# Moving one low half of weights per plain up tile to GpSimd, and setting the four convolution taps in one block

## The chip, the cores and the metric

The kernel runs on one core of one Trainium2 chip. The metric is the device time of one execution in microseconds (us), the median of several runs. Engines are named as in the profile: PE is TensorE (matmul), PEld its weight loads, DVE is VectorE, ACT is ScalarE, POOL is GpSimd, SP is SyncE. SP only issues DMAs here.

## The reference

A two-layer decoder trunk over 512 positions of width 1024. Layer 0 mixes positions with a gated MLP, layer 1 with sliding-window attention; both then run the same channel mixer, which is the part that the change touches, and a gated per-layer embedding. The channel mixer is a gated MLP with a causal depthwise convolution of width 3 between the up-projection and the activation; D_FF is 2816, so `w_up` has 5632 columns:

```python
def conv_ffn(xn, w_up, conv_w, conv_b, w_down):
    h = xn @ w_up
    hp = jnp.pad(h, ((0, 0), (CONV_WIDTH - 1, 0), (0, 0)))
    c = conv_b + sum(hp[:, t:t + S] * conv_w[t] for t in range(CONV_WIDTH))
    g, u = jnp.split(c, 2, axis=-1)
    return (jax.nn.silu(g) * u) @ w_down
...
for i in range(DEPTH):
    ...
    h = h + conv_ffn(rmsnorm(h, norm_ffn[i]), f_w_up[i], f_conv_w[i], f_conv_b[i], f_w_down[i])
```

Everything is float32, and the output is the normalised trunk, 512 x 1024.

## The kernel before, in words

**Products.** Each float32 product is made of three matmuls in the type fp32r: both operands are split into a high half (rounded to fp32r) and a low half (what is left), and the products high x high, high x low and low x high are added in PSUM. So every weight that TensorE uses must first be split.

**Weights.** All weights are planned ahead (L71 to L139) as a list of `pieces`, which are cut into `units` of at most 1024 columns. SP loads each piece into one of three raw buffers (`wraw`). `pump` (L179 to L206) prepares one unit after the other: ACT casts the high half (`wh`, L203), and then DVE subtracts, raw minus high, for the low half (`wl`, L204). There are four `wh` and four `wl` buffers (`WBUFS`), and whoever takes a unit first has units up to four ahead prepared. Some pieces are *woven*, that is, TensorE gets sums of quarters of the weights and so does seven products of half-size blocks where there were eight: for these, `weave` (L155 to L166) makes three sums on DVE in a buffer `wsum` (L163 to L165), and the piece has four units, three of up to 1024 columns and one of up to 512.

**The channel mixer** is `ffn` (L730 to L850). Its 22 up tiles (index j) are each 128 columns of the gate half and 128 of the other, for all 512 positions. They are worked in three parts: tiles 0 to 7, 8 to 15 and 16 to 21. Plain tiles are j = 0 to 6, 11, 13, 15 and 19, eleven to a layer: `up` (L737) takes two units, does 48 matmuls into two PSUM banks, and calls `gated` (L754). The other tiles are woven: `woven_up`, which ends in the same `gated`.

**`gated`** makes the convolution and the activation of a tile. For each half s: ACT writes `c_s`, the current position's tap with the bias, out of PSUM (L760); then DVE adds the two earlier positions, one instruction for each tap, which multiplies PSUM by a scalar and adds it to `c_s` (L762). Then ACT does silu of `c_0` (L768), and DVE multiplies by `c_1` (L769), which gives `a`.

**The end of a part.** Parts 0 and 1 close with the down-projection in woven form. Pairs of tiles are prepared by `Pair` (L504): sums of them on DVE (L518, L532 to L535), and their high and low halves `act` (the low halves on DVE at L312). Then TensorE runs first the next part's first up tile (8 or 16, woven; its two results are called `ux` and `uy`), without its `gated`, and after it `woven_add` (L593), whose two results are called `dx` and `dy` and whose first product uses `edge` and the first unit of `w_down`. That unit is number 59 at the end of part 0 and number 101 at the end of part 1; layer 1 has the same two ends with other numbers. Part 2 closes with plain products (`dense_add`). The last plain tile before the end of part 0 is tile 6 (tile 7 is woven), and before the end of part 1 it is tile 15.

**Order.** Nothing but the program sets the order on an engine: each engine runs its own list in the order in which the scheduler put it when the kernel was built, and waits, at an instruction, for whatever that instruction needs. `behind` holds an instruction behind another in that order, without a wait.

Of the kernel before, what the change touches and what calls it, by code (L numbers as in the profile page):

```python
# [8 lines left out]
F32 = mybir.dt.float32  # L9
F32R = mybir.dt.float32r  # L10
AF = mybir.ActivationFunctionType
ALU = mybir.AluOpType

P = 128
D = 1024
S = 512
# [36 lines left out]
def tile_yoco(ctx: ExitStack, tc: tile.TileContext, t, out: bass.AP, out_b: bass.AP):  # L53
# [83 lines left out]
                      [(ap, f"ah{q}", f"al{q}") for q in free[k0 : k0 + 4]] if c else None)  # L137

    units = [(i, q, lo, n) for i, p in enumerate(pieces) for q, (lo, n) in enumerate(p[2])]  # L139
    raws, ready, splits, sums = {}, {}, {}, {}  # L140
    state = {"raw": 0, "unit": 0, "next": 0, "tags": [0, 1, 2], "turn": 2, "pt": 0, "sent": {}}

    def behind(ins, front):

        tc.add_manual_dep(ins.ins, front.ins.name,
                          mybir.DependencyInfo(mybir.DependencyClass.NoSync, mybir.DependencyReason.DATA),
                          reason="order")

    def staged(name):
        tags = state["tags"]  # L150
# [28 lines left out]
    def pump(upto):  # L179
        while state["unit"] < min(upto, len(units)):  # L180
            i, q, lo, n = units[state["unit"]]
            load(i + 1)
            u = state["unit"]
            own = pieces[i][3]
            if own:
                pool, *tags = own[q]
                wh, wl = (pool.tile([P, n], F32R, tag=tg, name=f"own{u}_{tg}") for tg in tags)
            else:
                wh = wp.tile([P, UNIT], F32R, tag="wh", bufs=WBUFS, name=f"wh{u}")
                wl = wp.tile([P, UNIT], F32R, tag="wl", bufs=WBUFS, name=f"wl{u}")  # L190
            if i in woven:
                src = weave(i, q)
                hi, low = (x[:, :n].rearrange("p (b k m) -> p b k m", b=src.shape[1], m=P) for x in (wh, wl))
            elif i in paired:
                whole = raws[i][:, : pieces[i][1]].rearrange("p (c k n) -> p k c n", c=2, n=256)
                src = whole[:, lo // S : (lo + n) // S]
                hi, low = (x[:, :n].rearrange("p (k c n) -> p k c n", c=2, n=256) for x in (wh, wl))
            else:
                src, hi, low = raws[i][:, lo : lo + n], wh[:, :n], wl[:, :n]
            if u == 0:  # L200
                cast = nc.vector.tensor_copy(hi, src)
            else:
                cast = nc.scalar.copy(hi, src)  # L203
            state["split"] = splits[u] = cast, nc.vector.tensor_sub(low, src, hi.bitcast(F32))  # L204
            ready[u] = (wh, wl, n)
            state["unit"] += 1  # L206

# [74 lines left out]
    for i in range(IDLE):  # L282
        nc.tensor.matmul(ps, idle, idle.rearrange("p (o t) -> p o t", o=1).to_broadcast([P, 4, P]),
                         start=True, stop=True)
    minus_half = const.tile([P, S // 64], F32, name="minus_half")
    nc.vector.memset(minus_half, -0.5)
    ident = const.tile([P, P], F32, name="ident")
# [442 lines left out]
    def ffn(l, norm, nxt):  # L730
# [6 lines left out]
        def up(j, later=False):  # L737
            if j in UPS:
                return woven_up(j, later)
            parts = chunk(256, KD)  # L740
            pss = [psum(f"up{j}_{s}") for s in range(2)]
            if j:
                for s in range(2):
                    mm3(pss[s], parts, xs, s * P)
            else:
                for k, ((wh, wl, off), (xh, xl)) in enumerate(zip(parts, xs)):
                    for x, both in ((xh, (wh, wl)), (xl, (wh,))):
                        for s, ps in enumerate(pss):
                            for w in both:
                                nc.tensor.matmul(ps, w[:, off + s * P : off + (s + 1) * P], x,  # L750
                                                 start=k == 0 and x is xh and w is wh, stop=k == KD - 1 and x is xl)
            return pss if later else gated(j, pss)

        def gated(j, pss, fronts=()):  # L754
            cs = []
            for s, ps in enumerate(pss):
                col = s * NJ + j
                cw = [v("conv_w", (l * 3 + i) * 2 * NJ + col) for i in range(3)]
                c = tp.tile([P, S], F32, tag=f"c{s}", name=f"c{j}_{s}")
                nc.scalar.activation(c, ps, AF.Identity, bias=v("conv_b", l * 2 * NJ + col), scale=cw[2])  # L760
                for tap in (1, 2):
                    ins = nc.vector.scalar_tensor_tensor(c[:, tap:], ps[:, : S - tap], cw[2 - tap], c[:, tap:],  # L762
                                                         op0=ALU.mult, op1=ALU.add)
                    if fronts and tap == 1:
                        behind(ins, splits[fronts[s]][1])
                cs.append(c)
            a = tp.tile([P, S], F32, tag="sg", name=f"a{j}")
            box["silu"] = nc.scalar.activation(a, cs[0], AF.Silu)  # L768
            nc.vector.tensor_mul(a, a, cs[1])  # L769
            return a  # L770
# [866 lines left out]
```

## Time and profile before

| | |
|---|---|
| median of three runs | 1100.64 us (1100.06 to 1100.65) |
| span of the profiled execution | 1098.7 us |
| what the median is above the span | 1.9 us |
| PE busy | 1089.1 us (99%) |
| DVE busy | 959.0 us (87%) |
| ACT busy | 661.0 us (60%) |
| POOL busy | 125.0 us (11%) |
| instructions of PE, DVE, ACT, POOL | 6629, 1540, 1141, 192 |
| granted TensorE clock | full in each of 40 slices |

The profile is of one execution. Its span runs from the first instruction to the last; the time of an execution is taken outside of it. "Busy" is the time in which an engine has an instruction in work; matmuls follow each other in a pipeline and their ends overlap, so 99% says that TensorE nearly always had a next matmul, not that it was at its peak. A row of the timeline gives the start, the duration, engine, line and operation, output and inputs by the program's names without numbers, how many instructions were put together, and in brackets how long the engine was idle before them and what ended that. DVE's rows also overlap: the next instruction starts some 0.08 us before the row of the one ahead ends.

### The profile page before, as it was taken

What the parts mean: (1) busy time and instruction counts of PE and PEld (TensorE: products, weight loads), DVE (VectorE), ACT (ScalarE), POOL (GpSimd) and SP (SyncE); (2) the same over time, 40 slices, a digit from 0 to 9 for tenths busy, and PEclk for the clock granted to TensorE, in tenths of its full rate; (3) what the DMA queues carried; (4) which work ended last, traced back from release to release, by engine and by line L of the source; (5) the groups of instructions that cost most, each with busy time, mean ns of one, the idle gap of its engine ahead of it and who ended that gap; (6) DMA issues with size and microseconds to landing.
All of it is one profiled execution on the core that took longest, in us unless ns stands there. A gap on an engine that the chain in (4) does not pass through costs nothing.

```text
span 1098.7 us, 17476 instructions
## 1 busy us (share of the span) xinstructions
PE 1089.1 (99%) x6629; PEld 974.4 (89%) x6629; DVE 959.0 (87%) x1540; ACT 661.0 (60%) x1141; POOL 125.0 (11%) x192
## 2 busy tenths in 40 slices
PE   9999999999999999999999999999999999999997
PEld 7888988899998999988888887888999989999886
DVE  5588889999899989877988997799998999898887
ACT  5735666565676656655656775565655666567544
POOL 2200200000100010021114452000001000100200
PEclk9999999999999999999999999999999999999999
DMA  9621674125633267353234216441255333664534
GB/s 317 113 88 39 178 264 150 43 77 116 155 115 116 79 160 222 120 190 112 67 87 135 78 58 227 176 153 39 77 142 128 115 116 86 156 220 142 203 95 98
DMA packets 47508, 144.24 MB, mean 131 GB/s; under 512 B 13048, under 2 KB 18688, under 8 KB 36928
## 3 DMA queue, kind: packets, MB, share of 16 engines
q1 hardware_dynamic: 40560, 128.77, 35.6%
q0 software_dynamic: 5296, 9.70, 6.7%
q10 hardware_dynamic: 1568, 4.65, 1.1%
q8 instruction: 52, 0.85, 0.3%
q14 instruction: 32, 0.26, 0.1%
HBM read 116.89 MB, written 18.88 MB: 124 GB/s over the span
## 4 chain that ended last, share of the span: by engine, by line
PE 95%; DVE 2%; issue 1%; ACT 1%; DMA 0%; SPq 0%; POOLq 0%; POOL 0%; ACTq 0%
PE up L234 20%; PE ux L234 10%; PE dx L234 10%; PE uy L234 8%; PE dy L234 8%; PE d L234 6%; PE q L234 4%; PE gate L234 4%; PE u L234 4%; PE o L234 4%; PE up L750 2%; PE pv L1326 1%; PE v L244 1%; PE v L245 1%; PE v L246 1%; PE pin L234 1%
## 5 line engine op out<-in xcount | busy, mean ns | idle before, releaser
L204 DVE TENSOR_TENSOR wl<-wraw,wh 128x1024 fp32r<-128x1024 f32 (+2 forms) x198 | 217.3, 1102 | 42.8 <-ACT wh L203 41.9
L203 ACT CAST wh<-wraw 128x1024 fp32r<-128x1024 f32 (+2 forms) x197 | 182.8, 933 | 107.6 <-PE up L234 21.8
L203 ACT CAST wh<-wsum 128x1024 fp32r<-128x1024 f32 x84 | 88.3, 1052 | 62.7 <-issue 14.9
L204 DVE TENSOR_TENSOR wl<-wsum,wh 128x1024 fp32r<-128x1024 f32 x84 | 102.5, 1225 | 16.1 <-ACT wh L203 16.0
L762 DVE SCALAR_TENSOR_TENSOR c<-up,vec,c 128x511 f32<-128x511 f32 (+1 forms) x88 | 65.0, 744 | 2.4 <-ACT c L760 1.9
L234 PE MATMUL up<-nf10h,wh 128*128 128x512 f32 x160 | 62.3, 389 | 0.0
L234 PE MATMUL up<-nf00h,wh 128*128 128x512 f32 x160 | 62.3, 389 | 0.0
L234 PE MATMUL up<-nf10l,wh 128*128 128x512 f32 x160 | 62.3, 389 | 0.0
L234 PE MATMUL up<-nf00l,wh 128*128 128x512 f32 x160 | 62.3, 389 | 0.0
L234 PE MATMUL up<-nf00h,wl 128*128 128x512 f32 x160 | 62.1, 389 | 0.0
L234 PE MATMUL up<-nf10h,wl 128*128 128x512 f32 x160 | 62.0, 389 | 0.0
L600 POOL DMA_DIRECT2D saved<-head x16 | 13.9, 871 | 412.9 <-DVE head L720 412.9
L760 ACT ACTIVATE c<-up,vec 128x512 f32<-128x512 f32 x44 | 34.0, 777 | 31.8 <-PE up L234 26.6
L163 DVE TENSOR_TENSOR wsum<-wraw 128x1024 f32<-128x1024 f32 x42 | 51.2, 1220 | 0.6
L234 PE MATMUL ux<-t,wh 128*128 128x256 f32 x264 | 50.4, 283 | 0.0
L234 PEld LDWEIGHTS ux<-t,wh 128*128 128x128 f32 x264 | 41.2, 192 | 0.0
L234 PE MATMUL ux<-t,wl 128*128 128x256 f32 x132 | 37.4, 283 | 0.0
L234 PEld LDWEIGHTS up<-nf00h,wl 128*128 128x128 f32 x160 | 30.0, 188 | 6.2
L234 PEld LDWEIGHTS up<-nf10h,wl 128*128 128x128 f32 x160 | 30.0, 188 | 6.2
L234 PEld LDWEIGHTS up<-nf00l,wh 128*128 128x128 f32 x160 | 30.0, 188 | 6.2
L234 PEld LDWEIGHTS up<-nf10l,wh 128*128 128x128 f32 x160 | 30.0, 188 | 6.2
L234 PEld LDWEIGHTS up<-nf10h,wh 128*128 128x128 f32 x160 | 30.0, 188 | 6.0
(769 smaller groups left out, 3734.3 us busy)
## 6 DMA issues: line engine op xcount, KB each, us to landing
wraw<-in_w_up SPq DMA_DIRECT2D x44, 1024.0 KB, 5.6
wraw<-in_w_down SPq DMA_DIRECT2D x16, 1024.0 KB, 5.0
wraw<-in_w_gate SPq DMA_DIRECT2D x8, 1024.0 KB, 5.5
wraw<-in_w_down SPq DMA_DIRECT2D x8, 768.0 KB, 4.5
wraw<-in_w_u SPq DMA_DIRECT2D x4, 1024.0 KB, 9.4
wraw<-in_w_out SPq DMA_DIRECT2D x4, 1024.0 KB, 4.9
saved<-head POOLq DMA_DIRECT2D x16, 256.0 KB, 4.2
saved<-tail POOLq DMA_DIRECT2D x16, 256.0 KB, 4.1
```

The lines of the kernel that those rows point to most:

```text
L163: nc.vector.tensor_add(s[:, 0::3], g[:, 1:2].to_broadcast([P, 2, k, P]), g[:, 0::3])
L203: cast = nc.scalar.copy(hi, src)
L204: state["split"] = splits[u] = cast, nc.vector.tensor_sub(low, src, hi.bitcast(F32))
L234: return [nc.tensor.matmul(ps, w, x, start=first and j == 0, stop=last and j == len(todo) - 1, skip_group_check=onto) for j, (w, x) in enu ...
L244: nc.tensor.matmul(ps, xh[:, s], wh[:, a:b], start=st, stop=False)
L245: nc.tensor.matmul(ps, xl[:, s], wh[:, a:b], start=False, stop=False)
L246: nc.tensor.matmul(ps, xh[:, s], wl[:, a:b], start=False, stop=en)
L600: box["onto"] = nc.gpsimd.dma_start(x, y, accum_op=ALU.add)
L750: nc.tensor.matmul(ps, w[:, off + s * P : off + (s + 1) * P], x, start=k == 0 and x is xh and w is wh, stop=k == KD - 1 and x is xl)
L760: nc.scalar.activation(c, ps, AF.Identity, bias=v("conv_b", l * 2 * NJ + col), scale=cw[2])
L762: ins = nc.vector.scalar_tensor_tensor(c[:, tap:], ps[:, : S - tap], cw[2 - tap], c[:, tap:], op0=ALU.mult, op1=ALU.add)
L1326: nc.tensor.matmul(ps, lhs, rhs, start=j == 0, stop=j == len(todo) - 1)
```

## The change

In a plain up tile, the two halves of `gated` are taken together. ACT writes both `c_0` and `c_1` first. Then, at a higher priority for the scheduler, DVE copies one column of `c_1` to a small buffer `sign` (which nothing reads), and right behind it run the four taps in one block: first tap of `c_0`, first tap of `c_1`, second tap of `c_0`, second tap of `c_1`, each held behind the one ahead. One unit of weights that is prepared about then (the one that is two units beyond those which the tile has taken) gets its low half on GpSimd and not on VectorE, and this subtraction waits for the copy to `sign` with a semaphore. So 22 low halves of 128x1024, eleven in each layer, go from DVE to POOL, and DVE gets 22 copies of 128x1. Woven tiles keep the old `gated`.

```diff
+    def after(ins, front):
+
+        tc.add_manual_dep(ins.ins, front.ins.name,
+                          mybir.DependencyInfo(mybir.DependencyClass.Sync, mybir.DependencyReason.DATA),
+                          reason="start")
...
-            state["split"] = splits[u] = cast, nc.vector.tensor_sub(low, src, hi.bitcast(F32))
+            start = shadows.pop(u, None)
+            lows = (nc.gpsimd if start else nc.vector).tensor_sub(low, src, hi.bitcast(F32))
+            if start:
+                after(lows, start)
+            state["split"] = splits[u] = cast, lows
...
+    sign = const.tile([P, 1], F32, name="sign")
...
-            return pss if later else gated(j, pss)
-
-        def gated(j, pss, fronts=()):
+            return pss if later else gated(j, pss, shadow=True)
+
+        def gated(j, pss, fronts=(), shadow=False):
             cs = []
+            if shadow:
+                taps = []
+                for s, ps in enumerate(pss):
+                    col = s * NJ + j
+                    c = tp.tile([P, S], F32, tag=f"c{s}", name=f"c{j}_{s}")
+                    nc.scalar.activation(c, ps, AF.Identity, bias=v("conv_b", l * 2 * NJ + col),
+                                         scale=v("conv_w", (l * 3 + 2) * 2 * NJ + col))
+                    taps += [(c, ps, tap, v("conv_w", (l * 3 + 2 - tap) * 2 * NJ + col)) for tap in (1, 2)]
+                    cs.append(c)
+                with tc.high_priority():
+                    last = nc.vector.tensor_copy(sign, cs[1][:, :1])
+                    shadows[state["next"] + 2] = last
+                    for c, ps, tap, w in taps[::2] + taps[1::2]:
+                        ins = nc.vector.scalar_tensor_tensor(c[:, tap:], ps[:, : S - tap], w, c[:, tap:],
+                                                             op0=ALU.mult, op1=ALU.add)
+                        behind(ins, last)
+                        last = ins
+                a = tp.tile([P, S], F32, tag="sg", name=f"a{j}")
+                box["silu"] = nc.scalar.activation(a, cs[0], AF.Silu)
+                nc.vector.tensor_mul(a, a, cs[1])
+                return a
             for s, ps in enumerate(pss):
```

The line numbers shift with it: of what is named above, L163 to L165 become L169 to L171, L203 and L204 become L209 and L211, L312 becomes L323, L518 becomes L529, L532 to L535 become L543 to L546, L769 becomes L786 in a plain tile (L801 in a woven one). The copy is L777, the taps of the block are L780.

How DVE's list stands at two places. The names hold the tile (`c6_1` is the second half of tile 6, `act0_3_2` the third of the splits of pair 3 in part 0) or the unit (`wl59`), with a number behind it that is only a counter. The first place is DVE's list at the end of the last plain tile of part 0 in layer 0. Before:

```order
L762 SCALAR_TENSOR_TENSOR c6_0_2289<-up6_0_2239,vec_84,c6_0_2289 128x511
L312 TENSOR_TENSOR act0_2_2_2214<-act0_2u_2215,act0_2_2_2214 128x512
L762 SCALAR_TENSOR_TENSOR c6_0_2289<-up6_0_2239,vec_84,c6_0_2289 128x510
L204 TENSOR_TENSOR wl53_2309<-wsum26_2229,wh53_2308 128x1024
L204 TENSOR_TENSOR wl54_2313<-wraw26_2225,wh54_2312 128x512
L762 SCALAR_TENSOR_TENSOR c6_1_2293<-up6_1_2240,vec_84,c6_1_2293 128x511
L163 TENSOR_TENSOR wsum27_2345<-wraw27_2341 128x2x512
L762 SCALAR_TENSOR_TENSOR c6_1_2293<-up6_1_2240,vec_84,c6_1_2293 128x510
L164 TENSOR_TENSOR wsum27_2345<-wsum27_2345,wraw27_2341 128x512
L769 TENSOR_TENSOR a6_2297<-a6_2297,c6_1_2293 128x512
```

The same place on DVE in the changed kernel:

```order
L323 TENSOR_TENSOR act0_2_2_2221<-act0_2u_2222,act0_2_2_2221 128x512
L777 COPY sign_132<-c6_1_2298 128x1
L780 SCALAR_TENSOR_TENSOR c6_0_2296<-up6_0_2246,vec_84,c6_0_2296 128x511
L780 SCALAR_TENSOR_TENSOR c6_1_2298<-up6_1_2247,vec_84,c6_1_2298 128x511
L780 SCALAR_TENSOR_TENSOR c6_0_2296<-up6_0_2246,vec_84,c6_0_2296 128x510
L780 SCALAR_TENSOR_TENSOR c6_1_2298<-up6_1_2247,vec_84,c6_1_2298 128x510
L211 TENSOR_TENSOR wl54_2321<-wraw26_2232,wh54_2320 128x512
L786 TENSOR_TENSOR a6_2305<-a6_2305,c6_1_2298 128x512
L169 TENSOR_TENSOR wsum27_2353<-wraw27_2349 128x2x512
```

`wl53` has gone from DVE's list to POOL's. The two taps of `c6_0` and the half-size low `wl54`, which stood ahead of the first tap of `c6_1`, now stand with it or behind it.

The second place is DVE's list where the first units of the down-projection are prepared, at the end of part 0. Before:

```order
L312 TENSOR_TENSOR act0_3_0_2436<-a7_2433,act0_3_0_2436 128x512
L535 SCALAR_TENSOR_TENSOR act0_3u_2439<-act0_3u_2439,a7_2433 128x256
L312 TENSOR_TENSOR act0_3_1_2437<-act0_3t_2301,act0_3_1_2437 128x512
L204 TENSOR_TENSOR wl59_2486<-wraw28_2483,wh59_2485 128x1024
L312 TENSOR_TENSOR act0_3_2_2438<-act0_3u_2439,act0_3_2_2438 128x512
L204 TENSOR_TENSOR wl60_2520<-wsum28_2487,wh60_2519 128x1024
```

The same place on DVE in the changed kernel:

```order
L323 TENSOR_TENSOR act0_3_0_2444<-a7_2441,act0_3_0_2444 128x512
L546 SCALAR_TENSOR_TENSOR act0_3u_2447<-act0_3u_2447,a7_2441 128x256
L171 TENSOR_TENSOR wsum28_2495<-wsum28_2495,wraw28_2491 128x512
L323 TENSOR_TENSOR act0_3_1_2445<-act0_3t_2309,act0_3_1_2445 128x512
L323 TENSOR_TENSOR act0_3_2_2446<-act0_3u_2447,act0_3_2_2446 128x512
L211 TENSOR_TENSOR wl59_2494<-wraw28_2491,wh59_2493 128x1024
L211 TENSOR_TENSOR wl60_2528<-wsum28_2495,wh60_2527 128x1024
```

The split `act0_3_2` now stands ahead of `wl59`; the sum `wsum28` has only moved among work that stood ahead of `wl59` already. And at the end of part 1, on DVE before:

```order
L312 TENSOR_TENSOR act1_3_0_3843<-a15_3840,act1_3_0_3843 128x512
L535 SCALAR_TENSOR_TENSOR act1_3u_3846<-act1_3u_3846,a15_3840 128x256
L204 TENSOR_TENSOR wl101_3897<-wraw40_3894,wh101_3896 128x1024
L312 TENSOR_TENSOR act1_3_1_3844<-act1_3t_3775,act1_3_1_3844 128x512
L312 TENSOR_TENSOR act1_3_2_3845<-act1_3u_3846,act1_3_2_3845 128x512
```

There in the changed kernel:

```order
L323 TENSOR_TENSOR act1_3_0_3854<-a15_3851,act1_3_0_3854 128x512
L546 SCALAR_TENSOR_TENSOR act1_3u_3857<-act1_3u_3857,a15_3851 128x256
L323 TENSOR_TENSOR act1_3_1_3855<-act1_3t_3785,act1_3_1_3855 128x512
L170 TENSOR_TENSOR wsum40_3909<-wsum40_3909,wraw40_3905 128x512
L323 TENSOR_TENSOR act1_3_2_3856<-act1_3u_3857,act1_3_2_3856 128x512
L171 TENSOR_TENSOR wsum40_3909<-wsum40_3909,wraw40_3905 128x512
L211 TENSOR_TENSOR wl101_3908<-wraw40_3905,wh101_3907 128x1024
```

Here both splits `act1_3_1` and `act1_3_2` have moved ahead of the first unit's low half, `wl101`.

More of the change, by code (lines that the diff above doesn't have):

```diff
@@ L139, in tile_yoco @@
     units = [(i, q, lo, n) for i, p in enumerate(pieces) for q, (lo, n) in enumerate(p[2])]
-    raws, ready, splits, sums = {}, {}, {}, {}
+    raws, ready, splits, sums, shadows = {}, {}, {}, {}, {}
     state = {"raw": 0, "unit": 0, "next": 0, "tags": [0, 1, 2], "turn": 2, "pt": 0, "sent": {}}
```

## The prediction

> **What bounds the kernel now.** I read the page first: busy shares, and the shares of the chain that ended last.
>
> ```profile
> PE 1089.1 (99%) x6629; PEld 974.4 (89%) x6629; DVE 959.0 (87%) x1540; ACT 661.0 (60%) x1141; POOL 125.0 (11%) x192
> ...
> PE 95%; DVE 2%; issue 1%; ACT 1%; DMA 0%; SPq 0%; POOLq 0%; POOL 0%; ACTq 0%
> ```
>
> TensorE is the bound. So a shorter list on VectorE is worth only what TensorE waits for VectorE today. That is the view of the waits, for PE:
>
> ```profile
> PE idle L283 <- DVE minus_half L286: 1.1, 1, 1.1
> PE v L952 <- ACT n00h L307: 0.4, 1, 0.4
> PE uy L234 <- ACT side L805: 0.3, 2, 0.2
> ```
>
> The columns are us in total, times, longest. The first two are at the start of the program. No wait for a low half (L204) or for a tap (L762) is listed at all. Then I looked at where VectorE has room and where not, with busy times by stretch (start:end, length, PE, PEld, DVE, ACT and POOL busy, clock, DMA):
>
> ```profile
> 156.00:231.00 75.00, 75.00 (x338) 62.31 (x337) 70.05 (x111) 43.48 (x61) 0.00 (x0) 1.00 0.28 94
> 231.00:256.00 25.00, 24.85 (x207) 24.59 (x206) 24.68 (x37) 18.22 (x31) 0.00 (x0) 1.00 0.29 99
> 364.00:380.00 16.00, 16.00 (x134) 15.86 (x133) 15.22 (x23) 12.08 (x20) 0.00 (x0) 1.00 0.38 131
> ```
>
> The first stretch is the plain tiles of part 0 in layer 0: DVE has 5 us of room in 75, and PE none. The second is the end of part 0, from the last taps of tile 6 on: DVE is busy for 24.68 of 25.00 us. There VectorE has no room, and PE has all its work waiting behind what VectorE delivers. The third is the end of part 1. So the gain lies where nobody needs it, and the question is what the block of taps does to the two ends of parts in each layer.
>
> **What is removed.** VectorE loses 22 low halves and gains 22 copies:
>
> ```profile
> L204 DVE TENSOR_TENSOR wl<-wraw,wh 128x1024 fp32r<-128x1024 f32 x136 | 168.9, 1248 | 23.4 <-ACT wh L203 22.8
> L204 DVE TENSOR_TENSOR wl<-wsum,wh 128x1024 fp32r<-128x1024 f32 x84 | 102.5, 1225 | 16.1 <-ACT wh L203 16.0
> L762 DVE SCALAR_TENSOR_TENSOR c<-up,vec,c 128x511 f32<-128x511 f32 x44 | 32.6, 746 | 2.2 <-ACT c L760 1.9
> L1265 DVE DVE_READ_ACCUMULATOR2_ANT neg<- 128x1 f32 x64 | 5.0, 78 | 0.0
> ```
>
> 22 x 1.23 = 27 us of VectorE go; no copy of 128x1 is in the trace, and I price it by the nearest row of that shape, 0.08 us, so 22 x 0.08 = 1.8 us come (a full tap, 0.75, is the bound above, nothing the bound below). Net some 25 us of an engine that nobody waited for: worth 0 on the path. If the cover is wrong, the most to be had is the rows of waits above, under 2 us.
>
> **What GpSimd's low half costs.** The trace has no subtraction of 128x1024 on POOL. Its nearest rows, and what they do to VectorE beside them, are these (start, duration, engine):
>
> ```profile
> 537.90 1.29 POOL L342 TENSOR_TENSOR n1acc<-n1acc,n1sq 128x512 f32<-128x512 f32 x1 [3.84 <-ACT n1sq L337]
> 537.93 0.68 DVE L920 TENSOR_TENSOR z<-gate,np0rstd 128x512 f32<-128x512 f32 x1
> ...
> 523.36 1.34 POOL L342 TENSOR_TENSOR n1acc<-n1acc,n1sq 128x512 f32<-128x512 f32 x1 [3.85 <-ACT n1sq L337]
> 523.47 2.32 DVE L204 TENSOR_TENSOR wl<-wraw,wh 128x1024 fp32r<-128x1024 f32 x1
> ...
> 663.82 0.88 POOL L1341 TENSOR_TENSOR ol<-side,oh 128x128 fp32r<-128x128 f32 x2 [0.69 <-ACT oh L1340]
> ...
> L342 POOL TENSOR_TENSOR nf0acc<-nf0sq,nf0sq 128x512 f32<-128x512 f32 x1 | 1.7, 1722 | 0.0
> ...
> 166.10 2.73 DVE L762 SCALAR_TENSOR_TENSOR c<-up,vec,c 128x511 f32<-128x511 f32 x4 [0.67 <-ACT c L760]
> ```
>
> POOL's 128x512 took 1.29 us and its 128x128 some 0.44, so 0.85 / 384 = 2.2 ns for each further column, and 1024 columns are 1.29 + 512 x 0.0022 = 2.42 us (estimate). The bounds are 1.22 (as fast as VectorE's low half) and 2 x 1.72 = 3.44 (the slowest 512 row, twice). The second and fourth rows tell what VectorE suffers beside it: an operation that reads PSUM and SBUF (0.68) ran undisturbed, while a low half, which reads SBUF twice, took 2.32 in place of 1.22, about as long as POOL's operation and itself one after the other. The taps read PSUM, and four in a row took 2.73 us; POOL starts with the copy's end, so its 2.42 lies within them. I take it that it fits, at no cost; with 3.44 it would hold VectorE's next low half or sum by up to 0.8 us.
>
> The Trainium skill, "GPSIMD Engine Reference", Specifications, says the same of the port: VectorE is hindered in an instruction with two SBUF inputs; the trace agrees, 2.32 against 0.68. The same page of the Trainium skill speaks against the change under "Engine selection": elementwise work belongs on VectorE. By the page's table under "Elementwise" (4497 ns for an add of 2048 columns) the low half would be some 2.25 us, an estimate from that page, and the sum below would be the same.
>
> In the plain tiles a low half that comes 1.2 us later reaches nobody. The tightest is the last of a part, `wl53` after tile 6, a low half that VectorE begins at 228.02 and PE first uses at 235.66:
>
> ```profile
> 235.66 0.28 PE L234 MATMUL ux<-t,wl 128*128 128x256 f32 x1
> ```
>
> On POOL it starts with the block at 231.0 (below) and ends at 231.0 + 0.1 + 2.4 = 233.5, 2.1 us before that; with 3.44 still 1.1.
>
> **What the block moves.** At the end of tile 6, DVE's timeline before, and ACT's one row for the second half:
>
> ```profile
> 225.51 0.74 DVE L762 SCALAR_TENSOR_TENSOR c<-up,vec,c 128x511 f32<-128x511 f32 x1
> ...
> 226.77 0.74 DVE L762 SCALAR_TENSOR_TENSOR c<-up,vec,c 128x510 f32<-128x510 f32 x1
> 228.02 1.22 DVE L204 TENSOR_TENSOR wl<-wsum,wh 128x1024 fp32r<-128x1024 f32 x1 [0.51 <-ACT wh L203]
> 230.31 0.69 DVE L204 TENSOR_TENSOR wl<-wraw,wh 128x512 fp32r<-128x512 f32 x1 [1.06 <-ACT wh L203]
> 230.99 0.75 DVE L762 SCALAR_TENSOR_TENSOR c<-up,vec,c 128x511 f32<-128x511 f32 x1
> ...
> 230.18 0.77 ACT L760 ACTIVATE c<-up,vec 128x512 f32<-128x512 f32 x1
> ```
>
> VectorE waits twice here, 0.51 and 1.06 us, with `c6_0`'s taps already done: that is room which the block cannot use. `sign` needs `c6_1`, which ACT ends at 230.95, so the block starts at 230.99, where before only the last two taps were left. Four things now stand behind 230.99 which were done before it or after `wl59`: the copy, 0.08; `c6_0`'s two taps, 2.73 / 4 = 0.67 to 0.68 each, 1.33; the half-size low `wl54`, 0.60; and `act0_3_2`, 0.60, ahead of `wl59`. For 0.60 see the pace of two splits in the rows of part 1 below (372.41 to 373.01). The low that leaves, `wl53`, gives nothing back: it lay ahead of 230.99, beside the idle time. What follows to the down-projection's first unit:
>
> ```profile
> 239.62 1.22 DVE L204 TENSOR_TENSOR wl<-wsum,wh 128x1024 fp32r<-128x1024 f32 x1 [0.32 <-ACT wh L203]
> ...
> 249.17 1.21 DVE L204 TENSOR_TENSOR wl<-wraw,wh 128x1024 fp32r<-128x1024 f32 x1
> ...
> 250.78 0.28 PE L234 MATMUL dx<-edge,wl 128*128 128x256 f32 x1
> ```
>
> 249.17 is `wl59`, and PE needs it at 250.78, 0.40 us after its end. Between 230.99 and 249.17 VectorE is idle only once, for 0.32 us. So `wl59` moves to 249.17 + 0.08 + 1.33 + 0.60 + 0.60 - 0.32 = 251.46, ends at 252.67, and PE waits 252.67 - 250.78 = **1.9 us**. Nothing else on PE's list can run meanwhile, since it is in order.
>
> At the end of part 1 the block stands behind tile 15:
>
> ```profile
> 365.41 0.75 DVE L762 SCALAR_TENSOR_TENSOR c<-up,vec,c 128x511 f32<-128x511 f32 x1
> ...
> 371.28 1.22 DVE L204 TENSOR_TENSOR wl<-wraw,wh 128x1024 fp32r<-128x1024 f32 x1
> 372.41 0.68 DVE L312 TENSOR_TENSOR act<-act_3t,act 128x512 fp32r<-128x512 f32 x1
> 373.01 0.68 DVE L312 TENSOR_TENSOR act<-act_3u,act 128x512 fp32r<-128x512 f32 x1
> ...
> 374.77 0.28 PE L234 MATMUL dx<-edge,wl 128*128 128x256 f32 x1
> ```
>
> 371.28 is `wl101`. The additions are the same, with two splits in place of one: 371.28 + 0.08 + 1.33 + 0.60 + 2 x 0.60 = 374.49, ends at 375.71, and PE wants it at 374.77: 0.94, I take **1.0 us**. Here it stood 2.28 us ahead before.
>
> Layer 1 has the same two ends at the same distances:
>
> ```profile
> 796.99 1.22 DVE L204 TENSOR_TENSOR wl<-wraw,wh 128x1024 fp32r<-128x1024 f32 x1
> 798.60 0.28 PE L234 MATMUL dx<-edge,wl 128*128 128x256 f32 x1
> ...
> 919.10 1.22 DVE L204 TENSOR_TENSOR wl<-wraw,wh 128x1024 fp32r<-128x1024 f32 x1
> 922.60 0.28 PE L234 MATMUL dx<-edge,wl 128*128 128x256 f32 x1
> ```
>
> (0.39 and 2.28 us.) The sum is 2 x (1.9 + 1.0) = 5.8 us. On the profiled execution, 1098.7 becomes 1104.5; with the 1.9 us around the span, or straight from the median, 1100.64 + 5.8 = **1106.4 us**. After each wait PE's later needs are later by as much, so I count no second wait there.
>
> ACT's silu of a tile waits for the block's third tap, some 1.4 us later than before, and the casts behind it in ACT's list too. ACT is busy 18.22 of 25 us at that place, and its casts lead VectorE's subtractions, so I price this at 0; up to 0.5 at each end if it comes to lie behind the same wait.
>
> **The rivals.** *Nothing slips.* The list finishes in time all the same, say because the block runs faster than its rows or VectorE's waits in the block's tile were longer than the trace says. It decides at 0.40 + 0.32 = 0.72 us of added work at the first end, where I count 2.61, and at 2.28 for the second, where I count 3.21. Then the time is 1100.6, less at most a few tenths: 1099.8 to 1100.6. If only the first end slips, 2 x 1.9 gives 1104.4. For it speaks that the second end misses by 1 us alone; against it that the first is off by a factor of 3.6.
>
> *GpSimd's low half does not fit in the block.* Where it takes over 2.7 us, the half-size low or the sum behind the block waits for it as in the row at 523.47. At the four ends this adds 0.3 to 0.8 each (3.44 - 2.7 is the top): 1106.4 + 1.2 to 3.2 = 1107.6 to 1109.6. In the plain tiles it would be hidden. For it speaks that the margin is 0.3 us on an estimate.
>
> *TensorE's small waits go.* This is the other side, a gain. With 25 us less on VectorE, the casts, splits and results in front of PE come a little earlier everywhere, and the waits of the kind in the row at L805 go, while VectorE catches up at the ends (if what PE needs comes early enough there). The price is at most the rows of waits and the small gaps between matmuls, some 2 us: 1098.6. It decides where the additions at both ends stay under the margins, as for the first rival. Against it speaks that the freed time lies before tile 6's end, in a stretch where PE was busy 75.00 of 75.00 us.
>
> *It doesn't do what it says.* POOL's list holds the 22 low halves and DVE's the block, so this is only that the scheduler's gain is not where the edit is; it is in the first rival.
>
> **How the numbers follow.** A measurement of this kernel can tell about 0.2% from no change, 2.2 us: the borders are 1098.4 and 1102.8. Both ends slip, or the first alone: 0.66 (1104.4 to 1107.0). Nothing slips: 0.15. GpSimd doesn't fit: 0.12. The small waits go: 0.07. So faster 0.06 (the last case mostly falls below the border), same 0.16, slower 0.78. The range leaves out the gain and the top of GpSimd's case: 1100.3 to 1109.0.
>
> **What would show it.** DVE's timeline after would show the block of four taps at about 2.73 us, right behind a copy of 0.08, POOL's low half of about 2.4 beside it, `wl59` starting 2.3 us later against the start of its tile, and PE's waits would list a new row, `dx` for the low half at L211, four times, 1.9 and 1.0 us. Wrong is the step on the ends if that row is missing, the one on POOL if a low half or a sum behind the block is longer than 1.3 us, and the one on the plain tiles if PE waits for a low half there.

## The result and the profile after

| | before | after |
|---|---|---|
| median | 1100.57 us (1100.06 to 1100.65, 4 runs) | 1108.12 us (1107.68 to 1108.39, 4 runs) |
| span of the profiled execution | 1098.7 us | 1106.0 us |

The changed kernel takes 1.0067 times as long, with a 95% interval of 1.0055 to 1.0079: 7.5 us more. VectorE got its relief and TensorE lost time. The first line is from the page of the changed kernel, the next ones are PE's waits in it (us in total, times, longest):

```profile
PE 1090.5 (99%) x6629; PEld 974.4 (88%) x6629; DVE 933.4 (84%) x1540; ACT 660.2 (60%) x1141; POOL 179.0 (16%) x214
```

```profile
PE dx L244 <- DVE wl L211: 3.9, 4, 1.0
PE uy L244 <- ACT side L837: 1.4, 3, 0.6
...
PE dx L244 <- ACT head L713: 0.5, 1, 0.5
PE o L244 <- ACT oh L1372: 0.4, 1, 0.4
```

DVE is busy for 25.6 us less, POOL for 54 more. The first wait is new: four times `dx` for a low half, once at each end of a part. The second was there before with 0.3 us in two places. The last two are new as well, but neither lies at an end of a part (128.64 and 673.94 us). The three stretches of before, again by start:end, length, PE, PEld, DVE, ACT, POOL:

```profile
156.00:231.00 75.00, 75.00 (x336) 62.27 (x336) 60.99 (x107) 43.30 (x62) 14.46 (x6) 1.00 0.28 92
231.00:256.00 25.00, 23.41 (x192) 22.80 (x191) 24.74 (x38) 16.20 (x29) 2.41 (x1) 1.00 0.26 86
364.00:380.00 16.00, 15.05 (x117) 14.46 (x117) 13.93 (x23) 10.37 (x18) 2.42 (x1) 1.00 0.19 67
```

In the plain tiles PE is as full as it was and DVE has 9 us more room that nobody uses. At the end of part 0 DVE is still busy for 24.7 of 25 us, and now PE lacks 1.6 us. DVE's timeline there, from the copy behind tile 6 to the low half of unit 59, with POOL's and PE's rows:

```profile
228.87 0.69 DVE L323 TENSOR_TENSOR act<-act_2u,act 128x512 fp32r<-128x512 f32 x1 [1.19 <-ACT act L322]
231.26 0.15 DVE L777 COPY sign<-c 128x1 f32<-128x1 f32 x1 [1.70 <-ACT c L772]
231.33 2.71 DVE L780 SCALAR_TENSOR_TENSOR c<-up,vec,c 128x511 f32<-128x511 f32 x4
233.96 0.68 DVE L211 TENSOR_TENSOR wl<-wraw,wh 128x512 fp32r<-128x512 f32 x1
...
250.93 0.68 DVE L323 TENSOR_TENSOR act<-act_3u,act 128x512 fp32r<-128x512 f32 x1
251.53 1.22 DVE L211 TENSOR_TENSOR wl<-wraw,wh 128x1024 fp32r<-128x1024 f32 x1
```

```profile
231.56 2.41 POOL L211 TENSOR_TENSOR wl<-wsum,wh 128x1024 fp32r<-128x1024 f32 x1 [8.06 <-PE ux L244]
```

```profile
252.80 0.38 PE L244 MATMUL dx<-edge,wl 128*128 128x256 f32 x1 [0.98 <-DVE wl L211]
```

VectorE is idle for 1.19 and 1.70 us ahead of the copy, and then never again until the low half, which ends 0.05 us before PE's first matmul with it. At the end of part 1:

```profile
367.39 0.15 DVE L777 COPY sign<-c 128x1 f32<-128x1 f32 x1 [1.95 <-ACT c L772]
...
376.43 1.23 DVE L211 TENSOR_TENSOR wl<-wraw,wh 128x1024 fp32r<-128x1024 f32 x1
```

```profile
377.71 0.39 PE L244 MATMUL dx<-edge,wl 128*128 128x256 f32 x1 [0.95 <-DVE wl L211]
```

How much later PE comes to a unit than it did before can be read at the unit of the last plain tile (53, 99 and their twins) and at the second unit of the down-projection (60, 102 and their twins). The difference of the two is the loss at an end: 1.86, 1.08, 1.87 and 1.05 us, together 5.9 us of the 7.3 by which the span grew. At the end of part 0 the wait for the low half is only 0.98 of the 1.86; most of the rest is the wait for ACT's copy of the side result, which stands ahead of it on PE's list (0.61 us, where it was 0.15).

### The profile page after: what moved, and what is told of

It is laid out like the page before. It is cut to its first block, busy times and chain, and to the rows that moved or that the text cites. A ratio compares the mean times of both kernels' runs of the same rounds, so it can differ in the third digit from the quotient of the medians.

```text
span 1106.0 us, 17490 instructions
## 1 busy us (share of the span) xinstructions
PE 1090.5 (99%) x6629; PEld 974.4 (88%) x6629; DVE 933.4 (84%) x1540; ACT 660.2 (60%) x1141; POOL 179.0 (16%) x214
## 4 chain that ended last, share of the span: by engine, by line
PE 90%; DVE 6%; issue 2%; ACT 1%; DMA 1%; POOLq 0%; POOL 0%; SPq 0%; ACTq 0%; DVEq 0%
PE up L244 20%; PE dx L244 10%; PE ux L244 8%; PE dy L244 7%; PE uy L244 6%; PE d L244 6%; PE q L244 4%; PE gate L244 4%; PE u L244 4%; PE o L244 4%; PE up L761 2%; DVE wl L211 1%; PE pv L1358 1%; PE v L254 1%; PE v L255 1%
## 5 line engine op out<-in xcount | busy, mean ns | idle before, releaser
L209 ACT CAST wh<-wraw 128x1024 fp32r<-128x1024 f32 (+2 forms) x197 | 182.7, 933 | 118.9 <-PE up L244 20.3
L211 DVE TENSOR_TENSOR wl<-wraw,wh 128x1024 fp32r<-128x1024 f32 (+2 forms) x186 | 203.0, 1095 | 37.0 <-ACT wh L209 36.5
L209 ACT CAST wh<-wsum 128x1024 fp32r<-128x1024 f32 x84 | 88.3, 1051 | 59.8 <-DVE wsum L170 21.5
L211 DVE TENSOR_TENSOR wl<-wsum,wh 128x1024 fp32r<-128x1024 f32 x74 | 90.4, 1226 | 11.1 <-ACT wh L209 11.1
L780 DVE SCALAR_TENSOR_TENSOR c<-up,vec,c 128x511 f32<-128x511 f32 (+1 forms) x88 | 59.6, 740 | 0.0
L211 POOL TENSOR_TENSOR wl<-wsum,wh 128x1024 fp32r<-128x1024 f32 x10 | 24.1, 2412 | 213.6 <-PE ux L244 213.6
L169 DVE TENSOR_TENSOR wsum<-wraw 128x1024 f32<-128x1024 f32 x42 | 51.3, 1222 | 0.6
L211 POOL TENSOR_TENSOR wl<-wraw,wh 128x1024 fp32r<-128x1024 f32 x12 | 28.9, 2408 | 119.6 <-DVE sign L777 102.7
L244 PEld LDWEIGHTS up<-nf00h,wh 128*128 128x128 f32 x160 | 30.1, 188 | 6.0
```

Of the source, the lines that this page charges most:

```text
L169: nc.vector.tensor_add(s[:, 0::3], g[:, 1:2].to_broadcast([P, 2, k, P]), g[:, 0::3])
L211: lows = (nc.gpsimd if start else nc.vector).tensor_sub(low, src, hi.bitcast(F32))
L244: return [nc.tensor.matmul(ps, w, x, start=first and j == 0, stop=last and j == len(todo) - 1, skip_group_check=onto) for j, (w, x) in enu ...
```

## Experiments

(The expectations speak of 5.6 us at the ends and 1.7 elsewhere; the reading by units above gives 5.9 and 1.4. Some of them put 1.75 us on the low half at the end of part 0, where the trace has 0.98 for it and 0.61 for the copy of the side result.) The theory to be tested: the loss lies at the four ends, because the block cannot begin before the second half of tile 6 or 15 is there, and pushes VectorE's list behind what TensorE needs first. The rivals: each of the 22 blocks costs a little, or GpSimd's low halves cost VectorE time wherever they are. The kernel before ran beside each set on the same chip: median 1100.81 us for the first four, 1100.51 for the next three, then 1100.65 and 1100.79.

**All tiles but those at the ends.**

```diff
-            return pss if later else gated(j, pss, shadow=True)
+            return pss if later else gated(j, pss, shadow=j not in (6, 15))
```

> The block and GpSimd's low half are left out for tiles 6 and 15 alone (the last plain tiles before the ends of parts 0 and 1), 18 of 22 tiles keep them. Theory (the loss lies at the four ends, because the block cannot start before the second half of tile 6 or 15 and pushes the low half of the down-projection's first unit, 59 or 101, behind TensorE's need): the 5.6 us that the changed kernel's trace shows at the ends go, and at most the 1.7 us that lie elsewhere stay: 1100.6 to 1102.3. Rival (each of the 22 blocks costs a little, some 7.5 / 22 = 0.34 us each): 18 x 0.34, so 1106.7. Rival (GpSimd's low halves beside VectorE cost it, wherever they are): the same 1106.7.

Measured: 1101.77 us (1100.22 to 1103.19, 11 runs), ratio 1.0010 [1.0001, 1.0019]. Its waits for PE hold no low half any more:

```profile
...
PE dx L244 <- ACT head L713: 0.4, 2, 0.2
PE uy L244 <- ACT side L837: 0.2, 1, 0.2
```

So 18 blocks with their low halves on GpSimd cost 1.0 us together (0.1 to 2.1 by the interval), and neither rival's 6 us is there.

**Only the tiles at the ends.**

```diff
-            return pss if later else gated(j, pss, shadow=True)
+            return pss if later else gated(j, pss, shadow=j in (6, 15))
```

> The block and GpSimd's low half in tiles 6 and 15 alone, four of 22. Theory (ends): the whole 5.6 us of the ends, 1100.6 + 5.6 = 1106.2, between 1105.5 and 1107. Rival (a cost of each block or each low half): 4 x 0.34 = 1.4, so 1102.0.

Measured: 1106.84 us (1106.56 to 1107.02, 5 runs), ratio 1.0055 [1.0043, 1.0068], and the same new waits:

```profile
PE dx L244 <- DVE wl L211: 3.9, 4, 1.0
PE uy L244 <- ACT side L837: 1.2, 2, 0.6
...
```

Four blocks make 6.0 us. With the 1.0 of the other eighteen that is 7.0 of the 7.5.

**The block without GpSimd.** All 22 blocks and copies stay, and all low halves are on VectorE.

```diff
                     last = nc.vector.tensor_copy(sign, cs[1][:, :1])
-                    shadows[state["next"] + 2] = last
```

> The block and the copy in all 22 tiles, but all low halves on VectorE, none on GpSimd. VectorE's list now has the low halves of units 53 and 54 ahead of the block, in time in which it was idle, so of the four terms at the end of part 0 the 0.60 of the half-size low is gone. Theory (ends): the first unit's low half is 2.0 us later at the end of part 0 and 2.6 at the end of part 1, less 0.3 of idle time and the margins of 0.4 and 2.28: 1.3 and 0.35 us of waiting, twice: 1100.6 + 3.3 = 1103.9, between 1103 and 1105.5 with what lies elsewhere. Rival (GpSimd's low halves are the cost): 1100.6. Rival (the block with its place alone, whatever stands behind it): 1108.

Measured: 1104.74 us (1104.09 to 1104.96, 5 runs), ratio 1.0036 [1.0022, 1.0049]. PE's waits:

```profile
PE uy L244 <- ACT side L836: 2.3, 4, 0.6
...
PE dx L244 <- DVE wl L211: 0.5, 2, 0.3
...
```

So about half of the loss, 3.9 us, is the block's alone, with no GpSimd in it (2.4 to 5.4 by the interval). The half-size low behind the block is confirmed by its size: without it the wait for the low half of unit 59 is 0.3 us, where it was 1.0, and 0.60 were forecast for it. The end of part 1 is not: the expectation had 0.35 us for the low half there, and it was in time (the two waits that are left are those of part 0), but TensorE waited for ACT's copy of the side result instead. VectorE's list is late as a whole, and ACT's casts of the last pair's splits, which wait for it, stand ahead of that copy. PE's row and ACT's there:

```profile
373.38 0.39 PE L244 MATMUL uy<-nf00h,wh 128*128 128x256 f32 x1 [0.58 <-ACT side L836]
...
372.44 0.61 ACT L322 CAST act<-act_3t 128x512 fp32r<-128x512 f32 x1
372.96 0.36 ACT L836 COPY side<-uy 128x256 f32<-128x256 f32 x1
```

**GpSimd without the block.** The taps as in the kernel before, and each of the 22 low halves on GpSimd as soon as its cast is done.

```diff
-            if start:
-                after(lows, start)
...
-            return pss if later else gated(j, pss, shadow=True)
+            if not later:
+                shadows[state["next"] + 2] = True
+            return pss if later else gated(j, pss)
```

> The 22 low halves on GpSimd, but each as soon as its cast is there, with no wait for a copy, and the taps as in the kernel before, no block. Theory (ends): the first unit's low half stands where it stood, and GpSimd's port costs VectorE up to a microsecond beside each low half, in plain tiles, where nobody waits: 1100.6, within 1. Rival (GpSimd's low halves are the cost): 1105 or more, and without the taps as a cover more than the changed kernel, over 1108.

Measured: 1102.93 us (1102.43 to 1104.26, 10 runs), ratio 1.0021 [1.0012, 1.0030]: 2.1 us, twice what the theory allowed and half of the least that the rival wanted. PE's waits, and what GpSimd does to VectorE with no block beside it (two places, DVE's row and POOL's):

```profile
PE uy L242 <- ACT side L837: 0.7, 2, 0.3
PE up L759 <- DVE nf00l L450: 0.5, 1, 0.5
...
```

```profile
161.66 2.97 DVE L450 TENSOR_TENSOR nf00l<-h,nf00h 128x512 fp32r<-128x512 f32 x2
...
363.62 2.54 DVE L527 TENSOR_TENSOR act_3t<-a 128x256 f32<-128x256 f32 x1
366.09 0.41 DVE L528 TENSOR_TENSOR edge<-a,edge 128x256 fp32r<-128x256 f32 x1
```

```profile
161.07 2.40 POOL L211 TENSOR_TENSOR wl<-wraw,wh 128x1024 fp32r<-128x1024 f32 x1 [12.08 <-ACT wh L209]
...
363.49 2.40 POOL L211 TENSOR_TENSOR wl<-wsum,wh 128x1024 fp32r<-128x1024 f32 x1 [18.75 <-ACT wh L209]
```

An operation of 128x256 is held until GpSimd is done and takes 2.54 us; the next one of its size takes 0.41. The first pair of rows is tile 0's input being prepared, where TensorE waits for it. The second is at tile 15, just before the end of part 1, and there the hold does what the block does, only less of it: VectorE's list is late, and TensorE waits 0.34 us for ACT's copy of the side result, once in each layer (at 373.20 and 922.00 us, the first row of the waits above). So GpSimd's low halves without a cover do cost, at tile 0 and at the ends of part 1, less than the block does. And most of the hold is free here: by their rows, VectorE's operations beside the 22 low halves took 24.7 us longer in all than the same operations take elsewhere, for 2.1 us of time. In the changed kernel the same count is nothing: no VectorE row beside any of GpSimd's 22 low halves is longer than its kind, so the hold is no part of that kernel's loss.

**The first unit's low half early.** The changed kernel, with the four low halves of the down-projection's first units at a higher priority.

```diff
-    pieces, paired, woven, beside = [], set(), set(), set()
+    pieces, paired, woven, beside, firsts = [], set(), set(), set(), set()
...
+                firsts.add((len(pieces), 0))
                 plan_woven(t["w_down"][l], 4, j0, j1)
...
-            lows = (nc.gpsimd if start else nc.vector).tensor_sub(low, src, hi.bitcast(F32))
+            with tc.high_priority() if (i, q) in firsts else contextlib.nullcontext():
+                lows = (nc.gpsimd if start else nc.vector).tensor_sub(low, src, hi.bitcast(F32))
...
```

> The changed kernel with the low halves of the down-projection's first units (59, 101 and their two twins) early in VectorE's list: 59 ahead of the last taps of tile 7, 101 right behind the block of tile 15. If only that low half is late, the waits of 1.75 and 1.1 us for it go at both ends, and what stays is the wait for ACT's copy of the side result (0.77 less 0.31 before) and the rest: 1100.6 + 2 x 0.5 + 1.7 = 1103. Rival (all of VectorE's list is late at the ends; the splits of the last pair then come 1.1 us later, ACT's casts of them too, and the copy of the side result, which stands behind these casts in ACT's list, keeps PE waiting instead): the waits only change their name, 1107 to 1108.5.

Measured: 1102.32 us (1101.01 to 1103.24, 11 runs), ratio 1.0016 [1.0007, 1.0024]. 5.7 of the 7.5 us are gone, and the waits did not change their name; no row of `dx` or `uy` is left among PE's:

```profile
...
PE v L259 <- DVE wl L214: 0.3, 1, 0.3
PE sc L1293 <- PE sc L1294: 0.2, 1, 0.2
```

It is not a clean test of the low half alone, though. With the operand there early, the scheduler also put work with it ahead on PE's list. PE's timeline at the end of part 0 has `dx` from 249.71 on, and the products of `uy` that need the side result only at 252.60; in the changed kernel `uy` came first:

```profile
249.71 0.28 PE L247 MATMUL dx<-edge,wh 128*128 128x256 f32 x1
...
252.60 0.39 PE L247 MATMUL uy<-nf00h,wh 128*128 128x256 f32 x1
```

So the copy of the side result had 2.9 us of other work as a cover. Both waits went with one edit, and the run does not say what either was worth alone.

**The same in the kernel before,** as a control: the low half at L204 and the plan are edited likewise.

```diff
...
-            state["split"] = splits[u] = cast, nc.vector.tensor_sub(low, src, hi.bitcast(F32))
+            with tc.high_priority() if (i, q) in firsts else contextlib.nullcontext():
+                lows = nc.vector.tensor_sub(low, src, hi.bitcast(F32))
+            state["split"] = splits[u] = cast, lows
...
```

> The kernel before, with the same four low halves early in VectorE's list, as a control for the first of this set. If only these low halves matter: 1100.6, no change. Rival (the splits behind them matter as much, by ACT's copy of the side result, which waited 0.31 us at the end of part 0 already): up to 1.1 us at each of two ends, 1101.5 to 1103.

Measured: 1100.52 us (1099.84 to 1100.87, 11 runs), ratio 1.0002 [0.9993, 1.0011]. The early low halves are worth nothing where nothing is late.

**GpSimd at work for twice as long.** The changed kernel, with each of GpSimd's low halves done twice.

```diff
+            if start:
+                after(nc.gpsimd.tensor_sub(low, src, hi.bitcast(F32)), start)
             lows = (nc.gpsimd if start else nc.vector).tensor_sub(low, src, hi.bitcast(F32))
```

> The changed kernel with each of GpSimd's 22 low halves done twice in a row (the second writes the same), so that GpSimd is at work for about 4.8 us from the block's start, and the block covers 2.7 of them. If GpSimd holds VectorE's next two-SBUF operation until it is done, VectorE's list slips by another 1.7 to 2.4 us at each of the four ends: 1108.1 + 6.8 to 9.6 = 1115 to 1118, and the plain tiles cost nothing more. Rival (it is not held): only the low half of GpSimd itself comes later, some 0.5 us behind TensorE's need after tiles 6 and 15: 1110.

Measured: 1143.13 us (1138.22 to 1145.06, 5 runs), ratio 1.0372 [1.0348, 1.0397]: 42.6 us, where the expectations allowed 17.5 at most and 9.5. POOL's two rows after a tile in the middle of the part, DVE's at that time, and POOL's after tile 6; then PE's waits:

```profile
178.09 2.41 POOL L212 TENSOR_TENSOR wl<-wraw,wh 128x1024 fp32r<-128x1024 f32 x1 [5.41 <-issue]
180.58 4.00 POOL L213 TENSOR_TENSOR wl<-wraw,wh 128x1024 fp32r<-128x1024 f32 x1
...
238.99 7.54 POOL L213 TENSOR_TENSOR wl<-wsum,wh 128x1024 fp32r<-128x1024 f32 x1
```

```profile
182.35 2.50 DVE L545 TENSOR_TENSOR act_0t<-a,a 128x256 f32<-128x256 f32 x1
```

```profile
PE ux L246 <- POOL wl L213: 15.0, 12, 5.2
PE dx L246 <- DVE wl L213: 4.8, 4, 1.7
...
PE up L246 <- POOL wl L213: 2.3, 4, 0.8
...
```

VectorE is held, as expected (2.50 us for a 128x256), but so is GpSimd, which no expectation had: the first of its two operations, beside the taps, takes 2.40 to 2.42 us in all 22 tiles, the second, which starts when VectorE is already at work with two-SBUF operations, 2.78 to 4.01, and 7.54 after tile 6. Its low half then comes too late for TensorE, in the plain tiles or just behind them (the two waits for `POOL wl`, 17.3 us, 5.2 of them after tile 6).

**The first half's taps ahead of the copy.**

```diff
+                for c, ps, tap, w in taps[:2]:
+                    ahead = nc.vector.scalar_tensor_tensor(c[:, tap:], ps[:, : S - tap], w, c[:, tap:],
+                                                           op0=ALU.mult, op1=ALU.add)
                 with tc.high_priority():
                     last = nc.vector.tensor_copy(sign, cs[1][:, :1])
+                    behind(last, ahead)
                     shadows[state["next"] + 2] = last
-                    for c, ps, tap, w in taps[::2] + taps[1::2]:
+                    for c, ps, tap, w in taps[2:]:
```

> The changed kernel, but the two taps of a tile's first half run as soon as that half is there, ahead of the copy, in time in which VectorE was idle; only the second half's two taps stand behind the copy, and the half-size low of tiles 6 and 15 stands between them. GpSimd's low half still starts at the copy. If only VectorE's own work counted, the 1.33 us of these two taps would go from both ends: 1100.6 + 2 x (1.8 - 1.33 + 0) + 1.7 = 1103.2. If GpSimd's 2.41 us hold VectorE's next two-SBUF operation, the half-size low is not done before 2.7 us from the copy, so VectorE's list behind it starts as late as with four taps in the block, and the ends lose what they lost: 1107.5 to 1109, with the same waits of 1.75 and 1 us for the low halves of units 59 and 101.

Measured: 1133.84 us (1130.94 to 1135.40, 5 runs), ratio 1.0299 [1.0285, 1.0313]. Both expectations fail by 25 us or more. The hold is there; DVE's rows around a copy in a plain tile, and POOL's:

```profile
215.71 0.15 DVE L780 COPY sign<-c 128x1 f32<-128x1 f32 x1 [0.45 <-ACT c L772]
215.78 0.74 DVE L784 SCALAR_TENSOR_TENSOR c<-up,vec,c 128x511 f32<-128x511 f32 x1
216.44 3.04 DVE L211 TENSOR_TENSOR wl<-wraw,wh 128x1024 fp32r<-128x1024 f32 x1
219.40 0.74 DVE L784 SCALAR_TENSOR_TENSOR c<-up,vec,c 128x510 f32<-128x510 f32 x1
```

```profile
216.00 2.40 POOL L211 TENSOR_TENSOR wl<-wraw,wh 128x1024 fp32r<-128x1024 f32 x1 [9.66 <-DVE sign L780]
```

What was wrong is that it would be hidden in plain tiles. The scheduler had put a low half between the two taps. It was held for 1.8 us, and the second tap, `a` and ACT's casts of `a` with it. ACT's waits in this kernel, and the rows for the same two casts in the kernel before:

```profile
ACT act_0h L322 <- DVE a L790: 37.7, 10, 5.6
ACT edge L527 <- DVE a L790: 28.7, 8, 5.2
```

```profile
ACT edge L516 <- DVE a L769: 13.0, 9, 3.0
...
ACT act_0h L311 <- DVE a L769: 6.2, 4, 2.8
```

Behind that cast in ACT's list stand the next `c_0` and `c_1`, for which the next copy waits, and the copies of `ux` and `uy`. PE's largest waits here are for these (`uy` for the side result 12.2 us, `ux` for `out` 7.4); it never waits for GpSimd's low half itself.

Waiting is not all of the 33 us. In this run TensorE's granted clock fell to one half in three stretches, 13.7 us in all; here they are (start:end, length, then PE's busy time; the clock is the third figure from the end):

```profile
236.30:243.10 6.80, 5.66 (x26) 5.66 (x27) 6.49 (x8) 3.22 (x7) 2.38 (x1) 0.50 0.33 99
386.48:389.89 3.41, 3.41 (x18) 3.41 (x17) 3.41 (x5) 1.12 (x2) 0.00 (x0) 0.50 0.02 5
949.68:953.09 3.41, 3.41 (x19) 3.41 (x18) 3.41 (x5) 1.18 (x2) 0.00 (x0) 0.50 0.02 5
```

PE is busy for 12.5 us in them and does half as much, so some 6 us of the 33 are this (an estimate from these rows). The first stretch begins within a wait of 4.4 us, the others less than 1 us behind waits of 1.75; other waits here, of 2.9 and 3.0 us, had no such stretch behind them. GpSimd's doubled work above has three such stretches as well; for every other kernel here the records show half the clock in the last microseconds of the program alone. What brings such a stretch on was not tested.

**The same without GpSimd.** The last kernel, with all low halves on VectorE: the line `shadows[state["next"] + 2] = last` is left out.

> As the run before (the first half's two taps ahead of the copy, the second half's behind it), but all low halves on VectorE, none on GpSimd; the copies stay. It tells what made that run 33 us slower. If GpSimd held VectorE's low halves (3.04 in place of 1.22 us in its trace, 2.50 in place of 0.68) and through VectorE's list ACT's and TensorE's: all of it goes, and since the list at the ends then has only the copies more than the kernel before: 1100.6 to 1102. Rival (the new order of the taps itself, by the copy that waits for the second half): over 1125. This kernel is also the one that has neither of the two costs of the ends.

Measured: 1100.55 us (1099.74 to 1101.43, 11 runs), ratio 0.9999 [0.9990, 1.0008]. All 33 us came with GpSimd's low halves, and the copies and the order of these taps cost nothing that can be measured. It is also the second proof for the ends: its edit differs from the block without GpSimd only in the place of the first half's taps, and with them back in VectorE's idle time the 3.9 us are gone, and no wait for a low half is among PE's:

```profile
...
PE uy L244 <- ACT side L840: 0.3, 2, 0.2
...
```

No kernel beat the one before. PE's listed waits there come to 2.0 us, 1.1 of them at the program's start and 0.2 for TensorE's own work, so the rows show little that a lighter VectorE could have won.

## Why the prediction was right, point by point

It forecast 1106.4 us, slower, by both ends of parts in both layers; 1108.12 was measured, within the range.

- **TensorE is the bound and the 25 us of VectorE are worth nothing**: 25.6 us less DVE, and PE's time in the plain tiles of the first stretch as full as before. Shown.
- **The block starts with the second half.** Forecast at 230.99, the copy began at 231.26; all of PE's work stood 0.27 us later there from something before the first changed tile (below).
- **The added work at the end of part 0.** The sum put the low half of unit 59 at 20.47 us behind the block's start (251.46 less 230.99). It was 251.53 less 231.26, 20.27. PE's loss: 1.9 forecast, 1.86 and 1.87 measured. That it is so close is in part luck: the low half came 0.2 us earlier than forecast, and TensorE's restart, which the sum leaves out, made up for most of that (its first matmul starts 0.05 us behind the low half and takes 0.38 in place of 0.28). And the forecast row, `dx` for the low half with 1.9 us, shows 0.98: PE came to it later, by the wait for ACT's copy, and the low half, which ended last, set the sum.
- **The end of part 1.** From the block's start to the low half of unit 101, 9.08 us were forecast (374.49 less 365.41), and 376.43 less 367.39, 9.04, measured; loss 1.0 forecast, 1.08 and 1.05 measured.
- **Sum of the ends**: 5.8 forecast, 5.9 in the trace, 6.0 where the ends alone were changed.
- **The copy** at 0.08 us: its row is 0.15, and the next instruction starts 0.07 behind it, so the price of the list was right.
- **GpSimd's low half** at 2.42 us: 2.41. It fits in the block, but not by the 0.3 us of the forecast. GpSimd starts 0.15 us after the copy's row ends, so it ends at 233.97 where the next low half of VectorE starts at 233.96. It was a tie, and it held in all 22 tiles. What that rival says of the plain tiles, that a hold would be hidden there, is right only where nothing waits for what is held: 24.7 us of hold cost 2.1 us with the taps as before, but a hold between the two taps cost 33.
- **ACT's casts behind the block** at 0: too small a term, though not one that shows in the sum. At the end of part 0 PE waits some 0.6 us for ACT's copy of the side result (0.15 before) and 1.0 for the low half; without the low half it would be a loss of its own, as the block without GpSimd shows at the end of part 1.
- **What is missing from the sum**: 1.9 us from the forecast to the median. In the trace 1.4 us lie outside of the ends. The other eighteen tiles account for 1.0 by their own run. A part of the 1.4 may be this execution's alone: `dx` waiting for `head` L713, 0.5 us, is in the mixer ahead of the first changed tile, and in the runs above the same wait was 0.9, 0.2 or missing. Which of the small waits make the 1.0 was not separated.

The first rival, nothing slips, fell with the result and the first two experiments; the gain fell with the result, and no kernel here with a lighter VectorE went below the one before.

## What to carry to other kernels

When an engine that is not the bound gets a shorter list, look at where its list has no room, and ask what an added wait pushes behind that place: here 25 us were freed where nobody waited, and 2 us of work that had lain in idle time were moved into 18 us without any. Grouping instructions so that they begin when the last of their inputs is there gives up the idle time in which the earlier ones ran. And before work goes to GpSimd beside VectorE, measure what runs beside it: here four PSUM taps covered a low half and two did not. What a miss costs hangs on what stands behind the operation that is held: nearly nothing where that work has room, 33 us where TensorE's next results wait for it.

## What the runs showed of the hardware

- A VectorE operation with two SBUF inputs that begins while GpSimd's subtraction of 128x1024 is at work is held until that is done: 2.54 us in place of 0.41 for 128x256, 3.04 in place of 1.22 for 128x1024. The taps, which read PSUM and SBUF, ran beside it at 2.71 us for four, as without it (2.73). The Trainium skill, "GPSIMD Engine Reference", Key points, names such contention for instructions with two SBUF inputs; these rows agree.
- It goes both ways: GpSimd's own operation took 2.41 us beside the taps, and 2.78 to 4.01, once 7.54, where it started while VectorE was already at work with two SBUF inputs.
- A copy of one column on VectorE has a row of 0.15 us, and the next instruction begins 0.07 us after its start.
- In the two kernels in which TensorE waited longest, its granted clock was 0.50 in three stretches, 13.7 us in all, each within a wait or up to 1.4 us behind one; in the kernel before it fell so only in the last microseconds.
